# Four small reorderings in a two-layer DiT kernel: the transpose of the norm rows, one background step, the squaring of one MLP unit, and the low parts at the start of the last MLP

## The chip, the cores and the metric

The kernel runs on one core of one Trainium2 chip, in one launch. The metric is the device time of that core in microseconds; the kernel before was run three times, 1193.29, 1194.93 and 1197.53 us, median 1194.93. A compute engine executes its own instructions in order: TensorE (PE) does the matrix products and the transposes, VectorE (DVE), ScalarE (ACT) and GpSimd (POOL) the elementwise work, and SyncE (SP) issues nearly all loads. An instruction that needs another engine's result waits on a semaphore, and everything behind it on its engine waits with it.

## The reference, cut to what matters

Two transformer layers over 256 latent tokens `x` and 256 context tokens `ctx`, D = 1024. Each layer derives shifts, scales and gates from `c` (the adaLN weights `ada_w`, 25 MB a layer). Layer 0 mixes tokens with a chunked retention of 4 heads, layer 1 with neighbourhood attention of 32 heads; both are followed by a squared-relu MLP of width 4096. In layer 1 only the latents are needed.

```python
for i in range(DEPTH):
    mod = (silu_c @ ada_w[i] + ada_b[i])[:, None, :]
    mod_c = silu_cc @ ada_w[i] + ada_b[i]
    sh1, sc1, g1, sh2, sc2, g2 = jnp.split(mod, 6, axis=-1)
    h = x * (1.0 + sc1) + sh1
    hc = ctx * (1.0 + sc1c) + sh1c
    y, yc = retention_mixer(...) if i % 2 == 0 else neighbourhood_mixer(...)
    x = layer_norm(DN_ALPHA * x + g1 * y, ln_g[i, 0], ln_b[i, 0])
    h = x * (1.0 + sc2) + sh2
    x = layer_norm(DN_ALPHA * x + g2 * sq_relu_mlp(h, mlp_w1[i], mlp_w2[i]), ln_g[i, 1], ln_b[i, 1])
    # layer 0 does the same for ctx

def finish(o, g):      # the end of the retention: gates g, output weights w_o
    on = (of - mu) * lax.rsqrt(var + LN_EPS)
    return (on * jax.nn.silu(g)) @ w_o

def sq_relu_mlp(h, w1, w2):
    return jnp.square(jax.nn.relu(h @ w1)) @ w2
```

## The kernel before, in words

**Products.** Everything is fp32. A product is done as three matmuls of a reduced fp32 form: high part by high part, high by low, low by high (`mm3`). A weight unit of 512 KB is loaded by SP into one of four `raw` buffers (`fetch`), ACT casts it to `hi`, and DVE subtracts to get `lo` (`lows`; until then the cast is in the list `pending`). Only after `lo` is the raw buffer free for the next load. The adaLN chunks `rawa` take their buffers from the same four.

**Tokens.** 512 tokens stand in four tiles of 128: tiles 0 and 1 are latents, 2 and 3 context. Their transposed high and low parts are `hTh` and `hTl`.

**Order.** Each engine's calls go through `InOrder` (line 84, which is why every row of the profile says L84); where its switch is on, the engine's instructions keep the order of the program text, elsewhere a scheduler places them. PSUM has eight banks (`bank`), given out in turn: a new tile waits until the last reader of the bank's former tile is done.

**First stage.** While the first weights stream in, each of eight chunks `k` of the input is transposed, modulated and projected (`pq`, `pv`). `ln_columns` belongs to none of them: it transposes rows of norm weights and adaLN biases on PE (`pc`), copies them to `lnT` and `acol` on DVE, and stores a scaled copy through POOL. It stands in chunk 5.

**Retention heads.** For each head `h` the order on PE is q and k, v, scores, gates, states and outputs `po`, output projection `pw`. `gates((2, 3))` computes the gate inputs `pg` of the context tiles, `gate(0)` and `gate(1)` those of the latents. DVE normalizes `po` to `gs`, ACT makes silu's factor `sg` from `pg`, POOL multiplies (`gs<-sg,gs`), PE transposes the product (`pT`), ACT and DVE split it into `oh` and `ol` for `pw`. Beside it runs the background stream `bg()`: each step loads the next adaLN chunk on SP and weighs the one before with four `strips` instructions on DVE; after a group of chunks a reduction `red` and a small PE product `pada` give a group of columns. In head 0, each of the gate calls makes steps at k = 3: two until the first gate row is ready, one after.

**Layer 0's MLP.** Eight groups of hidden units (`fp`), each with two banks `p1` (a half of 128 hidden units each, latents in the left 256 columns, context in the right). The first two groups start on the latents alone, while the context tiles are still being normalized (`affine`, `mod_high`); then `evac1` squares the latents (relu on ACT, `scalar_tensor_tensor` on DVE into `r`, split into `hid` high and low), and `ctx_mm1` writes the context columns of the same banks.

**Layer 1's start of the MLP.** The last norm (`moments`, the reciprocal root on POOL, `shift_of`, `center` giving `xn`), the transposes `pt`, the affine that gives `hTh` and `hTl` (`affine_half` for tile 0, `direct` with `low1` for tile 1), and `tok_part`: the products of the first unit, tile by tile and part by part into `p00`, `p01`, `p10`, `p11` (`p1t` in the profile).

Of the kernel before, what the change touches and what calls it, by code (L numbers as in the profile page):

```python
# [19 lines left out]
KC = D // P  # L20
# [84 lines left out]
def kernel(  # L105
# [842 lines left out]
    w = ws[0]  # L948
# [8 lines left out]
    for k in range(KC):  # L957
        if k == 0:
            dt = slot(S_VL, [P, 4, 384], F32, "dt")
            sp.dma_start(out=dt[:, 0], in_=dist)  # L960
        if k == 3:
            sp.dma_start(out=cst1[:], in_=consts[:, NC0:])
            lrows = ln_rows()
        if k:
            chunk_q(k, ((0, 0),))
            part_v(k, 0, 0)
            chunk_q(k, ((1, 0), (0, 1)))
        if k < KC - 1:
            for i in range(2):
                chunk_sums(k + 1, i)  # L970
            chunk_turn(k + 1)
            ws[k + 1].high()
            chunk_row(k + 1)
            if k > 2:
                ws[k + 1].low()
        if k < 4:
            chunk_loads(k + 4)
        part_v(k, 1, 0)
        if k < KC - 1:
            chunk_columns(k + 1)  # L980
            chunk_modulate(k + 1, lambda: None if k > 2 else ws[k + 1].low())
        part_v(k, 0, 1)
        if k == 1:
            tabs = strip_tables(dt)
        if 1 < k < 6:
            make_strip(k - 2, *tabs)
        if k == 5:
            ln_columns(lrows)
        if k > 5:
            take(0, 2 * (k - 5))  # L990
# [54 lines left out]
    for h in range(RH):  # L1045
# [34 lines left out]
        def gates(ts, between=()):  # L1080

            pgs = [bank("pg") for _ in ts]
            for k in range(KC):
                wh, wl = gu[k // 2]
                for t, pg in zip(ts, pgs):
                    mm3(pg[:], hs(k, t * P, (t + 1) * P), (wh[:, k % 2, :], wl[:, k % 2, :]), k == 0, k == KC - 1)
                if h == 0 and k == 3:
                    bg(2 if G1s[0] is None else 1)
                    first_gate()
                if k in between:  # L1090
                    between[k]()
            return pgs
# [177 lines left out]
            stat(3, 1)  # L1270
            m3 = moments(3)

    def relu_sq(ps, sl, hh, hl):
        w = sl.stop - sl.start
        r = scr("r")
        act.activation(out=r[:, :w], in_=ps[:, sl], func=AF.Relu)
        dve.scalar_tensor_tensor(
            out=r[:, :w], in0=ps[:, sl], scalar=0.0, in1=r[:, :w], op0=ALU.max, op1=ALU.mult
        )
        split(r[:, :w], hh, hl)  # L1280


    HS = [S_T0, S_T1, S_SH, S_SL, S_TH, S_TL, S_GS, S_VH]
# [25 lines left out]
    for hf in range(2):  # L1309
# [9 lines left out]
        if hf == 0:  # L1319
            us = take(2, 2, 1)  # L1320
            pbs = [[bank("p1") for _ in range(2)] for _ in range(2)]
            hts = [hslot(fp) for fp in range(2)]
            mm1(us, LAT, pbs[0], range(0, 4))
            lows(1)
            shift = shift_of(*m3)
            f2 = affine(2, turn(2))
            fetch(1)
            low21 = mod_high(f2[1], 1, 2)
            white(3, shift, m3[1])
            low20 = mod_high(f2[0], 0, 2)  # L1330
            mm1(us, LAT, pbs[0], range(4, KC))
            lows(1)
            low21()
            us += take(2, 2)
            mm1(us[2:4], LAT, pbs[1], range(0, 4))
            p3 = turn(3)
            mm1(us[2:4], LAT, pbs[1], range(4, KC))
            f3 = affine(3, p3)
            low20()
            low31, low30 = (mod_high(f3[half], half, 3) for half in (1, 0))  # L1340
            low31()
            low30()
            take(0, 1)
            for fp in range(2):
                evac1(pbs[fp], LAT, hts[fp])
            for e in ORDER[1:]:
                e.on = False
            for fp in range(2):
                ctx_mm1(us[2 * fp : 2 * fp + 2], pbs[fp])
                evac1(pbs[fp], CTX, hts[fp])  # L1350
            hid += hts
            outside()
# [595 lines left out]
    settle_last(0, 1, wo_parts(0, 1))  # L1948
    mv0, r0 = moments(0)
    wo_first(1, 1, HALVES)  # L1950
    lows(1)
    fetch(1)
    shift = shift_of(mv0, r0)
    center(0, 0, mv0, r0, x0, shift)
    center(0, 1, mv0, r0, x0)
    fetch(1)
    settle_last(1, 0, wo_last(1, 0))

# [19 lines left out]
    def direct(pts, t):  # L1978
# [15 lines left out]
            part(half == 0, half, lambda k, i: hi[:, k])  # L1994

        def low(half):
            part(half == 1, half, lambda k, i: tmps[half][:, tsl(i)])
            ks = slice(4 * half, 4 * half + 4)
            dve.tensor_sub(
                out=lo[:, ks], in0=tmps[half][:].rearrange("p (k t) -> p k t", k=4), in1=hi[:, ks].bitcast(F32)  # L2000
            )
# [43 lines left out]
    HH, HL, LH = (0, 0), (0, 1), (1, 0)  # L2045
    tok_part(p00, 0, 0, *HH, LOW, start=True)
    tok_part(p00, 0, 0, *HL, LOW)
    tok_part(p00, 0, 0, *HH, HIGH)
    tok_part(p01, 0, 1, *HH, LOW, start=True)
    tok_part(p01, 0, 1, *HH, HIGH)  # L2050
    tok_part(p00, 0, 0, *LH, LOW)
    tok_part(p01, 0, 1, *LH, LOW)
# [14 lines left out]
    tok_part(p10, 1, 0, *HH, HIGH)  # L2067
    tok_part(p10, 1, 0, *HL, HIGH)
    tok_part(p01, 0, 1, *HL, LOW)
    low1(1)  # L2070
    lows(1)
    tok_part(p11, 1, 1, *HH, start=True)
    tok_part(p10, 1, 0, *LH, HIGH)
    tok_part(p01, 0, 1, *HL, HIGH, stop=True)
    low1(0)
    fetch(1)
    r00 = activate(p00)
# [166 lines left out]
```

## Time and profile before

| | |
|---|---|
| runs | 1193.29, 1194.93, 1197.53 us (median 1194.93) |
| profiled execution | 1193.21 us, its span 1191.4 us |
| granted TensorE clock | 0.998 |
| instructions | 17865 |
| bytes moved by DMA | 193.16 MB, mean 162 GB/s |

The profile shows one execution. A timeline row gives start and busy time in us, engine, line, operation, output and inputs by the program's names, and in square brackets the idle time of the engine just before it with what ended that. A row with x4 is four like instructions; its time is that of all four. The waits list gives total, times and longest. The stretches give length, then busy time and count for PE, PEld (PE's weight load), DVE, ACT and POOL, the clock, the DMA engines' share and GB/s.

### The profile page before, as it was taken

The page shows a single profiled execution, that of the slowest core. Times are in us where ns is not written, and L with a number is a line of the kernel's source. Part 1 is how long each engine was busy: PE and PEld are TensorE (multiplying, and loading weights), DVE is VectorE, ACT ScalarE, POOL GpSimd, SP SyncE. Part 2 cuts the span into 40 slices and gives each one's busy share as a digit, 9 for nine tenths or more (in the row PEclk, how much of TensorE's full clock was granted, in tenths as well). Part 3 has the DMA queues.
Part 4 walks back from the last instruction along what each step waited for, and adds up shares of the span by engine and source line. Part 5 has one row for each costly group of instructions (what it writes and reads, how often), then busy time and mean ns, then how long its engine had stood idle before and what let it go on. Part 6 is the DMA issues. An engine that isn't in the chain of part 4 may idle for free.

```text
span 1191.4 us, 17865 instructions
## 1 busy us (share of the span) xinstructions
PE 1175.3 (99%) x6884; PEld 987.6 (83%) x6884; DVE 833.5 (70%) x1308; ACT 479.4 (40%) x809; POOL 246.7 (21%) x389
## 2 busy tenths in 40 slices
PE   9999999999999999999999999999999999999997
PEld 7777888888888888888888888889778878999886
DVE  3776985777587477568867675578566688986446
ACT  3652232232223146442112333137466666666341
POOL 0103301310320141690203000123444431000001
PEclk9999999999999999999999999999999999999999
DMA  9964442444244115756566665556244334676661
GB/s 278 268 234 156 153 148 74 129 137 140 90 157 143 65 60 174 217 120 197 177 208 195 197 210 182 192 154 200 82 142 133 100 117 155 208 220 195 228 211 38
DMA packets 138041, 193.16 MB, mean 162 GB/s; under 512 B 9772, under 2 KB 81108, under 8 KB 137956
## 3 DMA queue, kind: packets, MB, share of 16 engines
q1 hardware_dynamic: 129572, 179.02, 47.3%
q0 software_dynamic: 7232, 10.44, 3.8%
q10 hardware_dynamic: 1152, 2.56, 0.7%
q8 instruction: 54, 0.88, 0.3%
q14 instruction: 31, 0.25, 0.1%
HBM read 187.15 MB, written 5.75 MB: 162 GB/s over the span
## 4 chain that ended last, share of the span: by engine, by line
PE 92%; DVE 3%; ACT 2%; issue 2%; POOL 1%; DMA 0%; DVEq 0%; POOLq 0%; ACTq 0%
PE p L84 43%; PE pq L84 8%; PE pv L84 7%; PE pw L84 7%; PE pg L84 7%; PE pn L84 5%; PE pnv L84 4%; PE po L84 2%; PE pada L84 2%; PE pS L84 1%; PE ppt L84 1%; PE pqk L84 1%; PE pav L84 1%; PE pt L84 1%; ACT s L84 1%
## 5 line engine op out<-in xcount | busy, mean ns | idle before, releaser
L84 ACT CAST hi<-raw 128x1024 fp32r<-128x1024 f32 (+2 forms) x228 | 232.6, 1033 | 323.7 <-PE p L84 117.7
L84 DVE TENSOR_TENSOR lo<-raw,hi 128x1024 fp32r<-128x1024 f32 (+2 forms) x228 | 279.8, 1238 | 94.1 <-ACT hi L84 93.3
L84 PE MATMUL p<-hi,hid 128*128 128x512 f32 (+1 forms) x832 | 241.7, 373 | 0.0
L84 PEld LDWEIGHTS p<-hi,hid 128*128 128x128 f32 x832 | 152.1, 188 | 27.6
L84 PE MATMUL p<-hTh,lo 128*128 128x256 f32 (+1 forms) x512 | 165.8, 326 | 0.0
L84 PE MATMUL p<-hTl,hi 128*128 128x256 f32 (+1 forms) x512 | 165.8, 326 | 0.0
L84 PE MATMUL p<-hTh,hi 128*128 128x256 f32 (+1 forms) x512 | 163.2, 328 | 2.5 <-DVE r L84 2.4
L84 PE MATMUL p<-lo,hid 128*128 128x512 f32 (+1 forms) x416 | 155.2, 373 | 0.0
L84 DVE SCALAR_TENSOR_TENSOR acc<-rawa,scol,acc 128x1024 f32<-128x1024 f32 x56 | 74.8, 1346 | 66.0 <-DMA rawa<-in_ada_w_dram 65.9
L84 PEld LDWEIGHTS p<-hTh,hi 128*128 128x128 f32 x512 | 94.2, 188 | 11.6 <-DVE r L84 2.9
L84 PEld LDWEIGHTS p<-hTh,lo 128*128 128x128 f32 x512 | 96.4, 188 | 8.8
L84 PEld LDWEIGHTS p<-hTl,hi 128*128 128x128 f32 x512 | 96.4, 188 | 8.7
L84 POOL TENSOR_TENSOR R<-R,acc 128x512 f32<-128x512 f32 x40 | 58.5, 1476 | 208.4 <-DVE acc L84 208.4
L84 PEld LDWEIGHTS p<-lo,hid 128*128 128x128 f32 x416 | 78.4, 188 | 13.7
L84 ACT CAST hid<-r 128x256 fp32r<-128x256 f32 (+1 forms) x64 | 31.9, 500 | 104.9 <-DVE r L84 104.9
L84 POOL TENSOR_TENSOR rstd<-rstd,misc 128x1 f32<-128x1 f32 x28 | 20.1, 718 | 213.3 <-DVE rstd L84 212.2
L84 DVE SCALAR_TENSOR_TENSOR strips<-rawa,scol,strips 128x512 f32<-128x512 f32 x84 | 61.4, 786 | 0.0
L84 ACT ACTIVATE s<-s,mn 128x512 f32<-128x512 f32 x64 | 45.5, 712 | 26.2 <-DVE mn L84 26.2
L84 PE MATMUL pg<-hi,hTh 128*128 128x512 f32 x128 | 51.4, 402 | 0.0
L84 PE MATMUL pw<-hi,oh 128*128 128x512 f32 x128 | 50.9, 398 | 0.0
L84 PE MATMUL pw<-hi,ol 128*128 128x512 f32 x128 | 50.1, 391 | 0.8 <-DVE ol L84 0.8
L84 PE MATMUL pg<-hi,hTl 128*128 128x512 f32 x128 | 50.0, 390 | 0.0
(238 smaller groups left out, 2281.1 us busy)
## 6 DMA issues: line engine op xcount, KB each, us to landing
raw<-in_mlp_w_dram SPq DMA_DIRECT2D x128, 512.0 KB, 4.4
rawa<-in_ada_w_dram SPq DMA_DIRECT2D x80, 512.0 KB, 4.2
raw<-in_ret_w_in_dram SPq DMA_DIRECT2D x42, 512.0 KB, 3.6
raw<-in_nat_w_in_dram SPq DMA_DIRECT2D x24, 512.0 KB, 4.0
rawq<-in_ada_w_dram SPq DMA_DIRECT2D x16, 512.0 KB, 6.0
raw<-in_ret_w_o_dram SPq DMA_DIRECT2D x16, 512.0 KB, 4.1
bias<-rpb_rows POOLq DMA_DIRECT2D x32, 128.0 KB, 2.9
raw<-in_nat_w_o_dram SPq DMA_DIRECT2D x8, 512.0 KB, 4.2
```

What stands on the lines that cost most here:

```text
L84: r = f(*args, **kwargs)
```

## The change

Four places.

1. `ln_columns` is called in the last chunk (k = 7) in place of chunk 5.
2. In head 0, `gates((2, 3))` makes no background step; `gate(0)` and `gate(1)` make two each as before. The number of steps in the program is the same, so the steps behind it each weigh the chunk that the step before them used to weigh.
3. `relu_sq` is cut in two: `squared` does the relu and the square, `split` follows. For the first group of layer 0's MLP, `squared` is called for both halves before `affine(3, ...)`, the split after it.
4. At layer 1's last norm, `lows(1)` moves behind the centring of tile 0; `low1` does its affine wholly on ACT; `p01`'s first part goes ahead of `p00`'s second, `p01`'s last part ahead of one of `p10`'s; and `lows(1)` goes ahead of `low1(1)`.

```diff
-        if k == 5:
+        if k == KC - 1:
             ln_columns(lrows)
...
-                if h == 0 and k == 3:
-                    bg(2 if G1s[0] is None else 1)
+                if h == 0 and k == 3 and len(ts) == 1:
+                    bg(2)
                     first_gate()
...
-    def relu_sq(ps, sl, hh, hl):
+    def squared(ps, sl):
         w = sl.stop - sl.start
         r = scr("r")
         act.activation(out=r[:, :w], in_=ps[:, sl], func=AF.Relu)
         dve.scalar_tensor_tensor(
             out=r[:, :w], in0=ps[:, sl], scalar=0.0, in1=r[:, :w], op0=ALU.max, op1=ALU.mult
         )
-        split(r[:, :w], hh, hl)
+        return r[:, :w]
+
+    def relu_sq(ps, sl, hh, hl):
+        split(squared(ps, sl), hh, hl)
...
             mm1(us[2:4], LAT, pbs[1], range(4, KC))
+            r0 = [squared(pb, LAT) for pb in pbs[0]]
             f3 = affine(3, p3)
...
-            for fp in range(2):
-                evac1(pbs[fp], LAT, hts[fp])
+            for i in range(2):
+                split(r0[i], hts[0][:, i, 0, LAT], hts[0][:, i, 1, LAT])
+            evac1(pbs[1], LAT, hts[1])
...
     wo_first(1, 1, HALVES)
-    lows(1)
     fetch(1)
     shift = shift_of(mv0, r0)
     center(0, 0, mv0, r0, x0, shift)
     center(0, 1, mv0, r0, x0)
+    lows(1)
     fetch(1)
...
         def low(half):
-            part(half == 1, half, lambda k, i: tmps[half][:, tsl(i)])
+            part(True, half, lambda k, i: tmps[half][:, tsl(i)])
...
     tok_part(p00, 0, 0, *HL, LOW)
+    tok_part(p01, 0, 1, *HH, LOW, start=True)
     tok_part(p00, 0, 0, *HH, HIGH)
-    tok_part(p01, 0, 1, *HH, LOW, start=True)
...
+    lows(1)
     low1(1)
-    lows(1)
     tok_part(p11, 1, 1, *HH, start=True)
+    tok_part(p01, 0, 1, *HL, HIGH, stop=True)
     tok_part(p10, 1, 0, *LH, HIGH)
-    tok_part(p01, 0, 1, *HL, HIGH, stop=True)
```

What stands in DVE's queue in head 0 at the gates of the context tiles, before (`strips` weigh the adaLN chunk `rawa`, `gs` is the normalized output, `lo` the low part of an output weight, `ol` the low part of the transposed product):

```order
L84 TENSOR_SCALAR gs_893<-po_1106,mv_1115,rstd_1117 128x512 [waits DVE_49,Pool_49]
L84 TENSOR_SCALAR strips_118<-rawa_1061,scol,strips_118 128x512 [waits DMAHW6_49]
L84 TENSOR_SCALAR strips_119<-rawa_1061,scol,strips_119 128x512
L84 TENSOR_SCALAR strips_118<-rawa_1061,scol,strips_118 128x512 [waits DVE_49]
L84 TENSOR_SCALAR strips_119<-rawa_1061,scol,strips_119 128x512 [waits DVE_49]
L84 TENSOR_TENSOR lo_1202<-raw_1199,hi_1201 128x1024 [waits DMAHW0_49,Activation_49]
L84 TENSOR_TENSOR lo_1208<-raw_1205,hi_1207 128x1024 [waits DMAHW1_49,Activation_49]
L84 TENSOR_TENSOR ol_1122<-pT_1161,oh_1121 128x4x128 [waits Activation_49]
```

And now:

```order
L84 TENSOR_SCALAR gs_893<-po_1106,mv_1115,rstd_1117 128x512 [waits DVE_49,Pool_49]
L84 TENSOR_TENSOR lo_1196<-raw_1193,hi_1195 128x1024 [waits DMAHW7_49,Activation_49]
L84 TENSOR_TENSOR lo_1202<-raw_1199,hi_1201 128x1024 [waits DMAHW0_49,Activation_49]
L84 TENSOR_TENSOR ol_1122<-pT_1155,oh_1121 128x4x128 [waits Activation_49]
L84 TENSOR_TENSOR lo_1208<-raw_1205,hi_1207 128x1024 [waits DMAHW1_49,Activation_49]
L84 TENSOR_TENSOR ol_1122<-pT_1168,oh_1121 128x4x128 [waits Activation_49]
L84 TENSOR_TENSOR lo_1214<-raw_1211,hi_1213 128x1024 [waits DMAHW2_49,PE_49,Activation_49]
```

The four strips of the chunk `rawa_1061` are gone from in front of the low parts; they come behind the last `ol` of this head.

DVE's queue around the affine of the fourth tile in layer 0's MLP, before (`aff` is the affine of a transposed tile, `r` the squared relu, `hid` its low part):

```order
L84 TENSOR_TENSOR hTl<-aff_3887,hTh 128x4x128 [waits Activation_49]
L84 TENSOR_SCALAR aff_3984<-pt_3950,AB_3591 128x128 [waits PE_49]
L84 TENSOR_SCALAR aff_3984<-pt_3950,AB_3591 128x128 x3
L84 TENSOR_TENSOR hTl<-aff_3882,hTh 128x4x128 [waits Activation_49]
L84 TENSOR_TENSOR hTl<-aff_3989,hTh 128x4x128 [waits Activation_49]
L84 TENSOR_TENSOR hTl<-aff_3984,hTh 128x4x128 [waits Activation_49]
L84 TENSOR_TENSOR lo_4002<-raw_3999,hi_4001 128x1024 [waits DMAHW7_49,Activation_49]
L84 TENSOR_SCALAR r_4005<-p_638_3839,r_4005 128x256 [waits Activation_49]
L84 TENSOR_TENSOR hid_3843<-r_4005,hid_3843 128x256 [waits Activation_49]
L84 TENSOR_SCALAR r_4010<-p_639_3840,r_4010 128x256 [waits Activation_49]
```

And now:

```order
L84 TENSOR_TENSOR hTl<-aff_3887,hTh 128x4x128 [waits Activation_49]
L84 TENSOR_SCALAR r_3984<-p_638_3839,r_3984 128x256 [waits Activation_49]
L84 TENSOR_SCALAR r_3987<-p_639_3840,r_3987 128x256 [waits Activation_49]
L84 TENSOR_SCALAR aff_3990<-pt_3950,AB_3591 128x128 [waits PE_49]
L84 TENSOR_SCALAR aff_3990<-pt_3950,AB_3591 128x128 x3
L84 TENSOR_TENSOR hTl<-aff_3882,hTh 128x4x128 [waits DVE_49]
L84 TENSOR_TENSOR hTl<-aff_3995,hTh 128x4x128 [waits Activation_49]
L84 TENSOR_TENSOR hTl<-aff_3990,hTh 128x4x128 [waits Activation_49]
L84 TENSOR_TENSOR lo_4008<-raw_4005,hi_4007 128x1024 [waits DMAHW7_49,Activation_49]
L84 TENSOR_TENSOR hid_3843<-r_3984,hid_3843 128x256 [waits Activation_49]
```

The two squarings `r` of the first group stand ahead of the affine of tile 3 and of a weight's low part, where they stood behind both; on ACT their relus go ahead of that engine's half of the affine likewise.

DVE's queue at the norm of tile 0 in layer 1, before (`mv` are the moments, `rstd` the argument of POOL's root, `nmr` the shift that needs the root's result):

```order
L84 TENSOR_SCALAR rstd_9042<-mv_9040 128x1 [waits DVE_49]
L84 TENSOR_TENSOR lo_9022<-raw_9019,hi_9021 128x1024 [waits DMAHW1_49,Activation_49]
L84 TENSOR_SCALAR nmr_9077<-mv_9040,rstd_9042 128x1 [waits Pool_49]
L84 TENSOR_SCALAR xn_8965<-R_104,mv_9040,rstd_9042 128x512
L84 TENSOR_TENSOR acc_9099<-pnw_9086,G_6873 128x512 [waits PE_49]
```

And now:

```order
L84 TENSOR_SCALAR rstd_9042<-mv_9040 128x1 [waits DVE_49]
L84 TENSOR_SCALAR nmr_9076<-mv_9040,rstd_9042 128x1 [waits Pool_49]
L84 TENSOR_SCALAR xn_8965<-R_104,mv_9040,rstd_9042 128x512
L84 TENSOR_TENSOR lo_9022<-raw_9019,hi_9021 128x1024 [waits DMAHW1_49,Activation_49]
L84 TENSOR_TENSOR acc_9099<-pnw_9086,G_6873 128x512 [waits PE_49]
```

The low part that stood between the root's argument and its first user now stands behind `xn`.

## The prediction, made before the changed kernel ran

> **What bounds the kernel now.** I read the page's table of busy times first: one engine is never free.
>
> ```profile
> PE 1175.3 (99%) x6884; PEld 987.6 (83%) x6884; DVE 833.5 (70%) x1308; ACT 479.4 (40%) x809; POOL 246.7 (21%) x389
> ```
>
> TensorE (PE) is busy 1175.3 of 1191.4 us, so the kernel gets faster by work taken from PE or by waits of PE that go. The change takes no matmul away; only waits are left. Next the list of what PE waited for (total, times, longest, in us):
>
> ```profile
> PE p L84 <- DVE r L84: 2.4, 1, 2.4
> PE pT L84 <- POOL gs L84: 1.5, 1, 1.5
> PE pw L84 <- DVE ol L84: 0.8, 1, 0.8
> PE pt L84 <- ACT xn L84: 0.6, 1, 0.6
> PE pc L84 <- PE pv L84: 0.5, 1, 0.5
> ```
>
> Each happens once; two waits of 0.3 and less for `p1t` follow further down. The timeline puts all seven into four stretches, so I asked for busy times by stretch (length, then busy time of PE, PEld, DVE, ACT, POOL, the clock, DMA share, GB/s):
>
> ```profile
> 49.00:76.00 27.00, 26.54 (x163) 19.92 (x161) 24.55 (x48) 18.41 (x28) 0.00 (x0) 1.00 0.77 245
> 76.00:105.00 29.00, 29.00 (x159) 21.91 (x158) 14.07 (x26) 6.94 (x10) 6.18 (x10) 1.00 0.60 203
> 105.00:121.00 16.00, 13.77 (x66) 10.75 (x65) 12.36 (x15) 5.89 (x8) 5.42 (x8) 1.00 0.39 132
> 121.00:450.00 329.00, 328.94 (x1534) 272.94 (x1533) 245.71 (x374) 97.83 (x142) 69.97 (x75) 1.00 0.37 119
> 450.00:468.00 18.00, 15.54 (x129) 15.13 (x128) 13.62 (x29) 12.40 (x25) 1.95 (x2) 1.00 0.41 140
> 468.00:990.00 522.00, 521.54 (x3079) 432.56 (x3078) 358.70 (x566) 217.57 (x408) 149.21 (x276) 1.00 0.55 168
> 990.00:1020.00 30.00, 28.83 (x207) 26.27 (x207) 26.80 (x51) 17.96 (x36) 2.42 (x2) 1.00 0.46 144
> 1020.00:1184.00 164.00, 163.92 (x1145) 152.18 (x1143) 106.55 (x142) 79.96 (x119) 3.99 (x3) 1.00 0.58 188
> ```
>
> Length less PE's busy time is PE's idle: 0.46, 2.23, 2.46 and 1.17 us in the four stretches that the change touches, 6.32 together. Between and behind them PE idles 0.00, 0.06, 0.46 and 0.08 us, so what is gained in one stretch is kept in the next as long as nobody else becomes late. A wait costs a little more than its idle time, because the overlap of successive matmuls is lost too:
>
> ```profile
> 112.11 0.39 PE L84 MATMUL pw<-hi,oh 128*128 128x512 f32 x1
> 112.33 0.39 PE L84 MATMUL pw<-lo,oh 128*128 128x512 f32 x1
> 113.48 0.50 PE L84 MATMUL pw<-hi,ol 128*128 128x512 f32 x1 [0.76 <-DVE ol L84]
> ```
>
> Starts are 0.22 apart while it runs and 1.15 at the wait: 0.93 lost where the row says 0.76, some 0.16 more. Seven waits make 1.1, so the ceiling of the whole change is about 7.4 us.
>
> **Part A, the norm rows' transpose two chunks later.** PE now waits 0.46 us for the PSUM bank of `pc`; with the 0.16 it is worth 0.62. Behind the last chunk the transpose stands between two projections and the bank has long been free. What is added: the copy to `lnT` and the two `acol` adds now stand in DVE's queue between the second and third of four low parts.
>
> ```profile
> 52.52 0.22 DVE L84 COPY lnT<-pc 128x64 f32<-128x64 f32 x1
> 52.66 0.26 DVE L84 TENSOR_SCALAR acol<-pc 128x24 f32<-128x24 f32 x2
> ```
>
> ```profile
> 77.93 1.23 DVE L84 TENSOR_TENSOR lo<-raw,hi 128x1024 fp32r<-128x1024 f32 x1 [1.81 <-ACT hi L84]
> ```
>
> The three take about 0.5 us by their starts, and DVE will wait a little for the transpose, an estimated 0.1, so everything behind them on DVE is some 0.6 later: two low parts, the rotation of q and k, and the loads that SP may issue only when DVE has freed a buffer. The cover is the 1.81 us that DVE idles before 77.93, and that PE idles 0.00 between 76 and 105 us; the last adaLN chunk's matmuls moreover stand four matmuls (0.9 us) later on PE. If that cover fails, the loss is at most the 0.6 us shift, which makes the part zero. Between 0 and 0.6 I take 0.4, nearer to the end that the 1.81 speaks for.
>
> **Part B, one background step fewer in head 0's gates of the context tiles.** The step loads an adaLN chunk on SP and weighs the previous one with four strips on DVE.
>
> ```profile
> 107.82 2.73 DVE L84 SCALAR_TENSOR_TENSOR strips<-rawa,scol,strips 128x512 f32<-128x512 f32 x4
> ```
>
> ```profile
> 114.05 1.05 ACT L84 CAST hi<-raw 128x1024 fp32r<-128x1024 f32 x1 [3.93 <-DMA raw<-in_ret_w_o_dram]
> 115.00 1.08 ACT L84 ACTIVATE sg<-pg 128x512 f32<-128x512 f32 x2
> ```
>
> ```profile
> 115.68 3.06 POOL L84 TENSOR_TENSOR gs<-sg,gs 128x512 f32<-128x512 f32 x2 [8.82 <-ACT sg L84]
> ```
>
> ```profile
> 216.83 2.55 POOL L84 TENSOR_TENSOR gs<-sg,gs 128x512 f32<-128x512 f32 x2 [7.30 <-ACT sg L84]
> ```
>
> ```profile
> 117.53 0.66 PE L84 MATMUL pT<-cst,gs 128*128 128x128 f32 x4 [1.47 <-POOL gs L84]
> ```
>
> Two chains hang on it. The strips delay the low parts and with them `ol`, for which PE waits 0.76. And they free the buffer into which SP loads the last output weight: ACT stands 3.93 us before its cast, both gate activations `sg` are queued behind that cast, POOL's product waits 8.82, and PE waits 1.47 for its transposes. Without the step that load takes the buffer of the chunk weighed one step before, and no longer waits for these strips; the gates run as soon as PE has finished them, which is before the 112.11 of the first `pw`. So `sg` starts near 111.6, over 3 us earlier, and the first product, half of the pair's 2.55 to 3.06, is done between 113.5 and 114. PE asks for it today at 117.53 less 1.47, and without the `ol` wait 0.93 earlier: 115.1. The dropped step falls to a later head, and every later step of the stream slides by one. Heads 1 to 3 already had the one-step order in these gates and show no wait there. Both waits with their restarts are 2.55; I take 2.4 and as the low end 0.9, only the `ol` wait.
>
> The product's two rows say what could hold it: the pair took 3.06 us in head 0, beside a low part on DVE, and 2.55 in head 1. The Trainium skill, "SBUF — State Buffer", section "Who interferes with whom", says that a DVE instruction with two SBUF inputs and a GpSimd one that reads SBUF exclude each other, the later one blocking fully; the trace agrees with a delay of that kind. By that rule the low parts that move next to the product could hold the first product for one whole low part, 1.2 us (the row at 77.93), to 115.2 at worst: level with PE's asking, and the sum would lose 0.1.
>
> **Part C, the first unit's latents squared ahead of tile 3's affine.** The largest single wait. PE wants to write the context columns of a bank of which DVE has still to read the latent columns.
>
> ```profile
> 460.67 2.44 PE L84 MATMUL p<-hTh,hi 128*128 128x256 f32 x16 [2.45 <-DVE r L84]
> ```
>
> ```profile
> 455.40 1.51 ACT L84 ACTIVATE aff<-pt,AB 128x128 f32<-128x128 f32 x4 [1.33 <-PE pt L84]
> 456.94 1.14 ACT L84 CAST hTh<-aff 128x512 fp32r<-128x512 f32 x2
> ```
>
> ```profile
> 455.07 1.36 DVE L84 TENSOR_SCALAR aff<-pt,AB 128x128 f32<-128x128 f32 x4
> ```
>
> ```profile
> 459.06 1.23 DVE L84 TENSOR_TENSOR lo<-raw,hi 128x1024 fp32r<-128x1024 f32 x1 [0.17 <-ACT hi L84]
> 460.20 0.42 DVE L84 SCALAR_TENSOR_TENSOR r<-p,r 128x256 f32<-128x256 f32 x1
> ```
>
> Reading DVE backwards: `r` at 460.20 stands behind a low part, which stands behind a cast, which stands behind the fourth tile's casts, none of which it needs. Now two relus (estimated as long as the squarings, 0.42 each) run on ACT in the 1.33 that it idles, and two squarings on DVE just ahead of its affine, which ends some 0.7 later, near 457.1; the second of the two casts starts only near 457.5 as it is. So the casts still end at 458.08; PE is ready at 460.67 less 2.45 and the restart, 458.06. What is left of the wait is nil to 0.1. The second unit's bank is asked for 48 matmuls later, some 7 us at the row's 0.15 each, and freed earlier than now. 2.45 plus 0.16, less 0.1: I take 2.45. The low end, if the squarings push the affine past the cast, is 1.75.
>
> **Part D, the start of the last MLP.** A single low part moves off POOL's reciprocal root, one affine goes from DVE to ACT, and PE takes parts whose operands are ready first.
>
> ```profile
> 997.89 1.50 POOL L84 TENSOR_TENSOR rstd<-rstd,misc 128x1 f32<-128x1 f32 x1 [11.88 <-DVE rstd L84]
> ```
>
> ```profile
> 403.80 0.57 POOL L84 TENSOR_TENSOR rstd<-rstd,misc 128x1 f32<-128x1 f32 x1
> ```
>
> ```profile
> 1000.54 1.09 PE L84 MATMUL pt<-cst,xn 128*128 128x128 f32 x8 [0.55 <-ACT xn L84]
> ```
>
> The same root takes 0.57 where DVE runs nothing beside it, so xn comes 0.9 earlier, more than the 0.55 that PE waits. The other waits in the stretch's 1.17, for `hTh` and `hTl` of `p1t`, are met by the order of the parts and by ACT's affine. With three restarts the 1.17 is about 1.7; I leave 0.1 for a rest at the last half: 1.6, low end 0.7 (the first wait alone).
>
> **Sum.** 0.4 + 2.4 + 2.45 + 1.6 = 6.85 us. The profiled execution took 1193.21, so the changed kernel's would take 1186.4. The median of the three runs is 1194.93, 1.72 above that; the predicted median is 1188.1.
>
> **Rivals.** (1) One of the two large waits stays or only moves. For C: the relus and squarings wait for matmuls of the second unit, and nothing is freed early; then 2.45 less, 1190.5. For B: ACT's casts still stand ahead of the gates; then 1.5 less, 1189.6. For it speaks that queues are in order and a single late item blocks all; against it that both chains have a margin of about 1 us. Chance 0.15. (2) The weights bind: the last MLP reads 188 GB/s, and the low part moved in D comes behind `xn`, an estimated 1.3 us later, and frees its buffer so much later. If the stream set the pace from there, D's 1.6 would become a loss of 1.3: 1191.0. Against it: the DMA engines' share there is 0.58, where the stretch from 49 to 76 moved 245 GB/s, and PE idles 0.08 in 164 us. Chance 0.05. (3) Slower: since the stream of steps slides by one, the adaLN columns of heads 1 and 2 stand directly ahead of PE's `po`, and DVE's queue behind them.
>
> ```profile
> 196.76 8.16 PE po L84 x36
> ```
>
> ```profile
> 191.16 0.17 DVE L84 TENSOR_TENSOR mod<-pada,acol 128x16 f32<-128x16 f32 x1 [3.47 <-PE pada L84]
> 191.25 0.87 DVE L84 TENSOR_SCALAR strips<-rawa,scol 128x512 f32<-128x512 f32 x2
> 192.04 4.06 DVE L84 SCALAR_TENSOR_TENSOR strips<-rawa,scol,strips 128x512 f32<-128x512 f32 x6
> 199.52 0.70 DVE L84 BATCH_NORM_STATS2 bs<-po 128x6 f32<-128x512 f32 x1 [3.42 <-PE po L84]
> ```
>
> Today `mod` runs at 191, eight strips follow, and DVE idles 3.42 before the first `bs`. Changed, the columns are turned where `po` starts, `mod` comes near 197.1, and one step's four strips follow, 0.8 us and a third of 4.06: 199.3, just in time for 199.52. If the chunk that they weigh lands late, `bs`, the products and PE follow one for one, twice. To eat 6.85 it must cost 3.4 in each head, that is land after some 201; to be slower by over 0.3% it must cost 5.2. Against it: the strips at 192.04 show no wait for their chunk today. Chance 0.05, time about 1199.
>
> **How the numbers follow.** The forecast has 0.75; 0.15, 0.05 and 0.05 go to the rivals. The range begins at the ceiling of 7.4 taken from a run 2 us under the median, 1185.0, and reaches over rivals (1) and (2) and the terms' low ends (0 + 0.9 + 1.75 + 0.7 = 3.35, which is 1191.6) to 1192.5. A measurement of this kernel can tell about 0.3%, 3.6 us, from no change, so faster means below 1191.3. The forecast, nearly all of it, and rival (1) fall there: 0.84. Rival (2) and several low ends at once are the same: 0.11. The rest is slower: 0.05.
>
> **What would show it.** Right: PE's waits for `r`, `gs`, `ol`, `xn` and `pc` gone from the list; idle in the four stretches under 1 us together; `sg` near 111; `r` for the first unit near 455.5 (less what was gained before); the root at 998 near 0.57. Wrong: a wait of PE for `pada` or `red` ahead of `po`; waits on loads in the last MLP; a PE wait for the hTh cast near 456 of more than 0.3; a new wait for adaLN chunks near 78.

## The result, and the profile after

The changed kernel takes 1186.26 us (median of 6 runs, 1185.87 to 1188.63), the kernel before, run beside it, 1194.24 (6 runs, 1193.29 to 1197.53): ratio 0.9935, 95% interval 0.9920 to 0.9951, 7.98 us less. The profiled execution is 1188.31 us, its span 1186.5; before it was 1193.21. So the medians fell by 8.0 and the profiled executions by only 4.9, and the reading has to explain both.

TensorE's list of waits is the first view again. These three rows are the whole list now; none is left of the seven that the change aimed at, and the three waits stood there before (the second with 0.4).

```profile
PE pq L84 <- DVE still L84: 1.2, 1, 1.2
PE pq L84 <- ACT hTh L84: 0.3, 1, 0.3
PE pqk L84 <- ACT pt L84: 0.3, 1, 0.3
```

The stretches agree (length, then busy time of PE, PEld, DVE, ACT, POOL, the clock, DMA share, GB/s). PE idles 0.00, 0.00, 0.00 and 0.14 us in the four places, where it idled 0.46, 2.23, 2.46 and 1.17.

```profile
49.00:76.00 27.00, 27.00 (x167) 20.10 (x170) 24.21 (x47) 18.60 (x28) 0.00 (x0) 1.00 0.78 245
104.50:118.00 13.50, 13.50 (x70) 11.18 (x68) 9.52 (x11) 5.90 (x8) 5.79 (x8) 1.00 0.45 146
440.00:468.00 28.00, 28.00 (x224) 27.41 (x223) 24.12 (x47) 20.91 (x39) 4.16 (x4) 1.00 0.51 151
980.00:1013.00 33.00, 32.86 (x258) 30.20 (x256) 29.75 (x57) 22.53 (x46) 1.50 (x2) 1.00 0.50 157
```

Where the time went is read best from the chain that ended last, by pieces that both kernels have (start, length, engine, output). They stand behind part A (head 0), behind B (heads 1 and 3), behind C (layer 0's MLP), ahead of D, and behind D (the last MLP). Before:

```profile
80.57 4.18 PE pS L84 x24
181.28 4.18 PE pS L84 x24
384.67 4.18 PE pS L84 x24
587.17 49.19 PE p L84 x216
813.84 14.54 PE pn L84 x120
1024.59 159.35 PE p L84 x1104
```

After:

```profile
80.16 4.18 PE pS L84 x24
178.06 4.18 PE pS L84 x24
381.45 4.18 PE pS L84 x24
580.98 49.19 PE p L84 x216
807.65 14.54 PE pn L84 x120
1016.92 162.12 PE p L84 x1104
```

The starts differ by 0.41, 3.22, 3.22, 6.19, 6.19 and 7.67 us. So A brought 0.41 in this execution, B 2.81, C 2.97 and D, by these pieces, 1.48; between the places less than 0.1 was gained or lost. Compared matmul by matmul, D brought 1.73 by 1017 us of before, just ahead of the last MLP's first product; the matmuls there are 7.85 earlier, and a slower pace takes 0.2 of that back by the last start. Then the last piece, the same 1104 matmuls, took 2.77 us longer. That alone makes 7.67 into 4.9; the experiments below show that it isn't the change's doing.

The moved instructions on the timeline (start, busy time, engine, operation, output and inputs, and in brackets the idle time before it). In head 0's gates of the context tiles the first gate activation, at 115.00 before, and POOL's product, at 115.68 before:

```profile
111.21 1.34 ACT L84 ACTIVATE sg<-pg 128x512 f32<-128x512 f32 x2 [0.99 <-PE pg L84]
111.89 2.55 POOL L84 TENSOR_TENSOR gs<-sg,gs 128x512 f32<-128x512 f32 x2 [5.44 <-ACT sg L84]
```

At the first unit of layer 0's MLP, relus and squarings in the gaps, and the cast that used to stand in front of them:

```profile
450.74 0.65 ACT L84 ACTIVATE r<-p 128x256 f32<-128x256 f32 x2
...
453.71 1.14 ACT L84 CAST hTh<-aff 128x512 fp32r<-128x512 f32 x2
```

```profile
451.83 0.75 DVE L84 SCALAR_TENSOR_TENSOR r<-p,r 128x256 f32<-128x256 f32 x2
452.50 1.36 DVE L84 TENSOR_SCALAR aff<-pt,AB 128x128 f32<-128x128 f32 x4
```

That cast was at 456.94: 3.23 earlier, all of what A and B had gained by then, so the squarings delay nothing. And the root of the last norm:

```profile
991.79 0.57 POOL L84 TENSOR_TENSOR rstd<-rstd,misc 128x1 f32<-128x1 f32 x1 [11.90 <-DVE rstd L84]
```

### The profile page after: what moved, and what is told of

It reads as the page before. It is cut to its first block, busy times and chain, and to the rows that moved or that the text cites. A ratio compares the mean times of both kernels' runs of the same rounds, so it can differ in the third digit from the quotient of the medians.

```text
span 1186.5 us, 17867 instructions
## 1 busy us (share of the span) xinstructions
PE 1176.7 (99%) x6884; PEld 990.9 (84%) x6884; DVE 832.8 (70%) x1304; ACT 480.9 (41%) x813; POOL 248.9 (21%) x389
## 4 chain that ended last, share of the span: by engine, by line
PE 96%; ACT 1%; DVE 1%; issue 1%; DMA 0%; POOL 0%; DVEq 0%; ACTq 0%
PE p L84 44%; PE pq L84 8%; PE pg L84 7%; PE pv L84 7%; PE pw L84 7%; PE pn L84 5%; PE pnv L84 4%; PE po L84 3%; PE pada L84 2%; PE pnw L84 1%; PE pS L84 1%; PE ppt L84 1%; PE pqk L84 1%; PE pt L84 1%; PE pav L84 1%; PE p1t L84 1%
## 5 line engine op out<-in xcount | busy, mean ns | idle before, releaser
L84 POOL TENSOR_TENSOR R<-R,acc 128x512 f32<-128x512 f32 x40 | 62.2, 1565 | 212.3 <-DVE acc L84 212.2
L84 DVE SCALAR_TENSOR_TENSOR strips<-rawa,scol,strips 128x512 f32<-128x512 f32 x84 | 66.4, 847 | 0.0
L84 PE MATMUL pg<-lo,hTh 128*128 128x512 f32 x128 | 50.0, 391 | 0.0
```

What stands on the lines that cost most here:

```text
L84: r = f(*args, **kwargs)
```

## The experiments

Of the single parts and of the whole I look at two things: the ratio of times, and the shift of PE's matmuls against the kernel before, matmul by matmul, just ahead of and just behind the place. Only the second tells parts of 0.4 to 3 us apart, because executions start up to 4.3 us apart. Most of that lies ahead of 20 us and goes with the granted clock, the share of full speed that TensorE's clock is allowed: its record has 1.00 from 5.4 us on in the profile of before, from 10.8 in that of C alone and from 17.6 in that of D alone, and at 20 us the latter two are 1.75 and 4.32 late.

### Each part alone

**A alone.**

```diff
-        if k == 5:
+        if k == KC - 1:
             ln_columns(lrows)
```

> Only the norm rows' transpose moved to the last chunk. Theory (the terms of the four parts add up, each by the PE wait it removes): PE's wait for pc (0.46 us, 0.62 with the restart) is gone, and PE reaches the second gate of head 0 about 0.4 us earlier than before; all other waits stay as before, the time falls by 0.4 us, too little to be told by time alone. Rival (the 0.6 us that DVE loses at 60 us comes back as a PE wait for the adaLN chunks near 76 to 79): gain 0 by 105 us.

1197.28 us against 1195.37, ratio 1.0009 (0.9998 to 1.0020): no gain. The wait for `pc` is gone and PE is 0.45 us earlier behind the moved transpose, at 62 us, but the list of waits has a row that wasn't there before:

```profile
PE pada L84 <- DMA rawa<-in_ada_w_dram: 0.2, 1, 0.2
```

By 105 us 0.24 is left of the 0.45.

**B alone.**

```diff
-                if h == 0 and k == 3:
-                    bg(2 if G1s[0] is None else 1)
+                if h == 0 and k == 3 and len(ts) == 1:
+                    bg(2)
```

> Only the background step in head 0's context gates dropped. Theory: PE's waits for ol (0.8) and gs (1.5) are both gone, PE is 2.4 to 2.8 us earlier at 130 us and keeps it to 450 us; the time falls by about 2.6 us. Rival 1 (POOL's product held by DVE's low parts): the gs wait shrinks but 0.5 us or more of it stays, gain under 2. Rival 2 (the slid background stream makes heads 1 and 2 late at po): a PE wait for red or po inputs near 196 and 298, gain at 450 us smaller than at 130 us.

1192.61 us, ratio 0.9980 (0.9967 to 0.9994). The waits for `ol` and `gs` are gone, and PE's shift goes from +1.54 at 101 us to -1.26 at 130: 2.80. It stays -1.26 up to 450 us, through `po` of heads 1 and 2, so the slid steps cost those heads nothing.

**C alone.** (`squared` for both halves ahead of `affine(3, p3)`, as in the change's diff.)

```diff
+            r0 = [squared(pb, LAT) for pb in pbs[0]]
             f3 = affine(3, p3)
```

> Only the first unit's latents squared ahead of tile 3's affine. Theory: PE's wait for r (2.4 us) is gone and none takes its place; PE is 2.5 to 3.0 us earlier at 480 us; the time falls by 2.5 to 3.0 us. Rival (the wait moves to the fourth tile's hTh cast or to the second unit's bank): a wait of 0.4 to 0.8 us stays near 458 or 464, gain under 2.2.

1191.74 us, ratio 0.9974 (0.9963 to 0.9985). The wait for `r` is gone, none takes its place, and the shift goes from +1.63 to -1.33: 2.96.

**D alone.** (All its edits at layer 1's last norm, as in the change's diff.)

```diff
-    lows(1)
     fetch(1)
...
     center(0, 1, mv0, r0, x0)
+    lows(1)
```

> Only the start of the last MLP reordered. Theory: the waits for xn, hTh and hTl are gone, POOL's root near 998 takes 0.55 to 0.6 us in place of 1.50, PE is 1.5 us earlier at 1022 us. In the stretch 1024 to 1094 us of 256-column matmuls the pitch of one matmul was 113.3 ns in the kernel before and 117.8 ns in the changed one. Theory 1 (the pitch is a state that varies from run to run, whatever the kernel): these four kernels show both values without relation to the edit. Theory 2 (the reordered start sets it): 117.8 here, 113.3 in the three kernels with the old start; then this kernel's time is 1.5 less 2.9, that is about 1.4 us slower than before.

1195.74 us, ratio 0.9991 (0.9978 to 1.0003): too small to be told by the time. In the trace the waits for `xn`, `hTl` and `hTh` are gone, and the shift goes from +5.40 to +3.67: 1.73.

### What makes each wait

**The dropped step behind the gates instead of nowhere.** The step is kept in head 0, but made after both products of the gates.

```diff
-                if h == 0 and k == 3:
-                    bg(2 if G1s[0] is None else 1)
+                if h == 0 and k == 3 and len(ts) == 1:
+                    bg(2)
...
+        if h == 0:
+            bg(1)
```

> Kernel before, but head 0's step of the context gates is made behind the gates and their products in the program, not left out: DVE's strips stand behind both ol, SP's order of loads stays. It separates the two chains of part B. Theory (the strips hold ol; the buffer that they free holds the third output weight, its cast, sg and POOL's product): the ol wait (0.8) goes, the gs wait stays, 1.0 to 1.8 us, since the third load now waits for the first low part's buffer, near 109, and PE asks for gs 0.9 earlier; PE is 0.9 to 1.4 us earlier at 130 us, about half of the 2.8 of the step dropped. Rival (DVE's queue is all there is to it, the load doesn't matter): both waits go, 2.8 us at 130 us.

1195.62 us in one execution; PE ends 0.42 us behind at 130, where 0.9 to 1.4 ahead was expected: a miss, but one that shows how the queue works. The first `ol` is early as foreseen, and PE is 0.92 ahead at 113. The load of the last output weight now waits for the buffer of the first low part and goes out at 109.57 instead of 110.58; ACT's cast still stands 4.28 us for it, with the gates behind it, so the wait for `gs` stays. And the four strips now stand in front of the third `ol`. DVE's rows, and PE's:

```profile
115.96 4.19 DVE L84 SCALAR_TENSOR_TENSOR strips<-rawa,scol,strips 128x512 f32<-128x512 f32 x4
121.81 0.68 DVE L84 TENSOR_TENSOR ol<-pT,oh 128x512 fp32r<-128x512 f32 x1
```

```profile
116.63 0.66 PE L84 MATMUL pT<-cst,gs 128*128 128x128 f32 x4 [1.13 <-POOL gs L84]
122.54 0.50 PE L84 MATMUL pw<-hi,ol 128*128 128x512 f32 x1 [1.60 <-DVE ol L84]
```

So the strips in DVE's queue and the load in ACT's are two separate chains, as part B had them, and moving the step just behind the gates isn't enough.

**The context columns in banks of their own.** Nothing is squared earlier; the matmuls that waited write elsewhere.

```diff
-                ctx_mm1(us[2 * fp : 2 * fp + 2], pbs[fp])
-                evac1(pbs[fp], CTX, hts[fp])
+                pbc = [bank("p1") for _ in range(2)]
+                ctx_mm1(us[2 * fp : 2 * fp + 2], pbc)
+                evac1(pbc, CTX, hts[fp])
```

> Kernel before, nothing moved, but the context columns of the first two groups of layer 0's MLP go to PSUM banks of their own. Theory (PE waits at 458 us for the readers of the bank, not for data): the wait for r is gone or under 0.2 us, PE is 2.6 to 4.1 us earlier at 470 us, as with the squaring moved. Rival (PE waits for the high parts of the fourth tile or for DVE as such): a wait of 1 us or more stays at 458 us.

1196.59 us in one execution, whose start was 4.2 late. The wait for `r` is gone with `r` as late as ever, and the shift goes from +6.27 to +3.31: 2.96, the same as for C alone. (Of the +6.27, 2.04 were lost at head 0's wait for `gs`, which lasted 1.98 in this execution; the edit doesn't touch that place.) The wait was for the bank, not for data.

**Half of D: only `lows(1)` behind the centring of tile 0.**

```diff
-    lows(1)
     fetch(1)
     shift = shift_of(mv0, r0)
     center(0, 0, mv0, r0, x0, shift)
     center(0, 1, mv0, r0, x0)
+    lows(1)
```

> Only one of the edits at the last norm: the single low part moved from beside POOL's reciprocal root to behind the centring. Theory (a low part on DVE holds the root): the root near 998 takes 0.55 to 0.60 us in place of 1.50, the wait for xn (0.5 to 0.6) is gone, the two waits for p1t stay, PE is 0.7 to 0.8 us earlier at 1002 us and no more at 1018. Rival (the root's length has another cause): it stays near 1.5, and PE gains nothing.

**The other half: all of D but that line** (`low1`'s affine on ACT and the order of the parts).

```diff
-            part(half == 1, half, lambda k, i: tmps[half][:, tsl(i)])
+            part(True, half, lambda k, i: tmps[half][:, tsl(i)])
...
```

> The edits at the last norm without the moved low part: ACT's affine, the order of the products' parts, and the last low part ahead of low1. Theory (each removes its own wait): the root near 998 takes about 1.5 us again and PE waits 0.5 to 0.6 for xn; the waits for hTh (0.2) and hTl (0.3) are gone, PE is 0.7 to 1.0 us earlier at 1022 us than at 1000 us, compared with the kernel before; with d_root's 0.76 this makes the 1.6 to 1.7 of all edits together. Rival (the parts need each other: without the earlier root the later waits come back): under 0.4 us.

One execution each, 1196.89 and 1194.01 us. POOL's root, in the first and in the second:

```profile
999.36 0.57 POOL L84 TENSOR_TENSOR rstd<-rstd,misc 128x1 f32<-128x1 f32 x1 [11.89 <-DVE rstd L84]
```

```profile
999.48 1.50 POOL L84 TENSOR_TENSOR rstd<-rstd,misc 128x1 f32<-128x1 f32 x1 [11.90 <-DVE rstd L84]
```

With the low part gone from beside it the root takes 0.57 and PE's wait for `xn` goes: PE gains 0.76 by 1002 us. Without that edit the root and that wait stay and the waits for `hTl` and `hTh` go. Read at 1017 us, ahead of the last MLP's first product, the halves bring 0.74 and 0.97; the two make 1.71, D alone made 1.73.

### The whole, with and without part A

**The changed kernel again**, for a comparison on one chip with the next kernels.

> The changed kernel once more, for its time beside the kernel before in many runs, and for a second profile. Theory (the four waits are gone for good, with them the fall of the granted clock at 460 us; what is left between runs is the start and the pitch of 113.3 or 117.8 ns in the last MLP): 7.5 to 9 us less than before by the medians, a ratio of 0.9925 to 0.994, no PE wait over 0.4 us behind the first 15 us, no clock under 1.00 near 455 us. If the pitch is 113.3 this time, PE ends some 7.7 us earlier than in the profile of before, less what the start differs. Rival (the changed start of the last MLP brings the pitch of 117.8 with it): 117.8 again, though the edit alone had 113.3.

1187.17 us (1186.99 to 1190.90, 5 runs), ratio 0.9940 (0.9928 to 0.9953), as expected. Two expectations failed: PE waits 1.0 us for an adaLN chunk near 79 us, and in the profile its last product starts 6.0 us earlier than before, not 7.7. The pace of the last MLP is the fast one this time.

**The change without A.**

```diff
-        if k == KC - 1:
+        if k == 5:
             ln_columns(lrows)
```

> The changed kernel with the norm rows' transpose left in chunk 5. Theory (part A is worth its wait, 0.4 to 0.5 us, and nothing else): PE's wait for pc is there again (0.4 to 0.5), PE is 0.2 to 0.5 us later at 130 us than in the changed kernel for the same start, and the time is 0.2 to 0.5 us above it, within the noise. Rival (DVE's lost 0.6 us at 60 us costs PE an adaLN wait in many runs, as in the one profile of the edit alone): the time is the same or lower than the changed kernel's, by up to 0.5 us.

1186.04 us (1185.79 to 1186.37), ratio 0.9926 (0.9912 to 0.9939). The ratios' intervals overlap, but each of its five runs is below each of the five with A: the version with A takes 1.1 us longer here. That is the rival's direction, and more than the 0.5 that it allowed. Between the two profiles lie 1.3 us. By the shifts 0.15 of it was there at 49 us, 0.6 comes at part A's place, and 0.55 at 776 us, where only the profile with A has a wait of PE for a low part; whether that one has to do with A is open. In the profile with A, PE's matmuls of the fourth chunk of adaLN's weights:

```profile
79.96 0.64 PE L84 MATMUL pada<-rawa,cT 128*32 128x256 f32 x8 [1.04 <-DMA rawa<-in_ada_w_dram]
```

and before, without a wait:

```profile
78.33 0.64 PE L84 MATMUL pada<-rawa,cT 128*32 128x256 f32 x8
```

The cause is seen on SP's queue (start and time, the loads with like ones put together). With A, and then before:

```profile
72.50 0.38 SPq L84 DMA_DIRECT2D raw<-in_ret_w_o_dram  x1
72.97 8.88 SPq L84 DMA_DIRECT2D rawa<-in_ada_w_dram  x5
```

```profile
71.69 0.38 SPq L84 DMA_DIRECT2D raw<-in_ret_w_o_dram  x1
72.88 7.36 SPq L84 DMA_DIRECT2D rawa<-in_ada_w_dram  x5
```

The output weight's load goes out 0.81 later, right in front of the chunk's load, because the two have changed the buffers that they wait for. Before, the first was released by a low part on DVE at 71.68 and the second by PE's adaLN matmuls at 72.87. With A the first waits for PE's adaLN matmuls, until 72.49; the low part on DVE was done at 72.16, so the second follows at once. (Why the buffers change places is open.) The chunk is issued 0.09 later but lands, by the trace, at 79.92 in place of 78.07: 6.95 us under way instead of 5.2. The same is seen in all three profiles with the transpose in the last chunk: the two loads go out 0.47 apart and the chunk takes 5.82, 6.09 and 6.95 us, where in the other eleven they go out 1.2 apart and it takes 4.64 to 5.56. Before, PE asked for it 0.26 us after its landing; there was no more margin than that. In the first profile of the changed kernel the chunk landed at 78.80 and PE asked at 78.86: just in time, hence the 0.41 there.

**The rows turned after head 0's second gate** (a third place for A's step, far from the loads).

```diff
-        if k == 5:
-            ln_columns(lrows)
...
+            ln_columns(lrows)   # behind gate(1) of head 0
```

> The changed kernel with part A's call put elsewhere: the norm rows are transposed behind head 0's second gate, at about 92 us, where DVE is about half idle, and neither in chunk 5 nor in chunk 7. Theory (part A removes PE's wait for pc but pays by DVE's 0.5 to 0.6 us at 60 us, which bunches the loads so that the adaLN chunk that PE asks for at 78 lands late): no wait for pc, no wait for rawa at 78 us beyond 0.1, PE 0.4 to 0.6 us earlier at 105 us than in the kernel before for the same start; about 0.4 us below the kernel without part A, a ratio of 0.992 to 0.9925. Rival (the wait of 1.0 us for rawa came by chance and can come in any kernel): a wait for rawa of 0.2 to 1.0 us near 78 us here as well.

1186.12 us (1185.66 to 1188.73, 6 runs), ratio 0.9926 (0.9911 to 0.9942). Neither the wait for `pc` at 50 us nor the one for the chunk is there, the two loads go out 1.20 apart again, and PE gains 0.46 by 105 us. The time doesn't show it: the same as without A within the scatter, where 0.4 less was expected. By their ratios these two versions are the best that ran, though the intervals overlap with the changed kernel's.

### The clock behind the wait

**Twenty idle matmuls in the wait for `r`**: the wait stays, but PE is not idle in it. The matmuls write a bank that nobody reads.

```diff
+            fill = bank("fill")
+            for _ in range(20):
+                pe.matmul(fill[:, LAT], lhsT=us[0][0][:, 0, tsl(0)], rhs=hTh[:, 0, LAT], start=True, stop=True)
```

> Kernel before with 20 idle matmuls (256 columns, result unused) put where PE waits 2.45 us for r at 458 us; the wait's reason is untouched. In the kernel before and three others with this wait the granted clock fell after it: 0.5 in the records, a pitch of 213 to 222 ns for 2 to 14 matmuls in place of 120; in the two kernels without the wait it did not. Theory (PE's idleness lowers the clock): no matmul slower than 125 ns after the filled stretch, PE 0.3 to 1.4 us earlier at 470 us than in the kernels with the wait, although it still starts the context columns no earlier than 460.7 less shifts. Rival (the slow matmuls come from DVE and ACT reading banks at that time): the pitch near 213 stays.

1195.25 us against 1197.42, ratio 0.9991 (0.9972 to 1.0011): not told apart by the time. The traces say why it was tried. With part A alone, where the wait is as before, the two microseconds behind it have a granted clock of 0.50 (the third figure from the end):

```profile
461.00:463.00 2.00, 2.00 (x11) 2.00 (x11) 1.52 (x4) 0.94 (x3) 0.28 (x1) 0.50 0.78 216
```

and with the idle matmuls

```profile
461.00:463.00 2.00, 1.99 (x15) 1.78 (x16) 1.26 (x4) 1.21 (x4) 0.01 (x1) 1.00 0.61 182
```

Six of the seven profiles with the wait show the clock fall to 0.50 behind it: 11 to 14 matmuls start every 0.21 us instead of 0.12, and PE loses 1.0 to 1.4 us. The profile of before is the seventh, without a fall; the expectation above wrongly counts it among the others. None of the seven profiles in which PE has no idle there shows it, the one with the idle matmuls included.

Why one profile escapes can be read off the traces. Each fall in the middle of a kernel lasts 3.41 us in the clock's record, and from the first record at 1.00 to a fall it is a whole number of times 3.413 us (453.97, or 133 times, with A alone). So the clock is set for one window of 3.41 us after another, and the windows' edges lie elsewhere in each execution. Cut at these edges, the stretches around the wait with A alone, around the same wait before, and around head 0's wait for `gs` with D alone (the figure behind the length is PE's busy time):

```profile
456.83:460.24 3.41, 1.31 (x11) 1.10 (x10) 2.67 (x5) 2.37 (x4) 0.00 (x0) 1.00 0.20 68
460.24:463.65 3.41, 3.07 (x14) 3.07 (x15) 2.00 (x6) 2.01 (x6) 0.52 (x1) 0.50 0.54 154
```

```profile
455.98:459.39 3.41, 2.24 (x19) 2.04 (x17) 2.68 (x6) 3.29 (x7) 0.00 (x0) 1.00 0.43 141
459.39:462.81 3.42, 2.12 (x15) 1.92 (x16) 2.48 (x6) 1.38 (x4) 0.00 (x1) 1.00 0.35 108
```

```profile
119.97:123.38 3.41, 1.87 (x11) 1.34 (x10) 2.22 (x2) 2.07 (x3) 3.06 (x2) 1.00 0.77 251
123.38:126.80 3.42, 3.42 (x19) 2.84 (x18) 3.05 (x5) 0.59 (x1) 1.98 (x2) 1.00 0.52 175
```

With A alone most of the wait falls into one window, PE is busy for 1.31 us of it, and the next window is at 0.50. Before, counted from its record at 5.42 us, an edge at 459.39 cuts the wait in two, and neither half is enough. In all fourteen profiles, between 16 and 1170 us, seven windows have PE busy for 1.50 us or less, and each is followed by one at 0.50; no other is, and the least busy of the others has 1.87. One of the seven is head 0's wait for `gs` in the run with other banks, 1.98 us long.

### The longer last piece

No kernel was made for this; all fourteen profiles answer. In the last MLP's first product, 256-column matmuls one after another, the stretch from 1030 to 1080 us of before, of after, and of the changed kernel run again:

```profile
1030.00:1080.00 50.00, 50.00 (x444) 50.00 (x443) 41.50 (x62) 32.27 (x58) 0.00 (x0) 1.00 0.67 211
```

```profile
1030.00:1080.00 50.00, 50.00 (x426) 50.00 (x426) 38.20 (x57) 30.32 (x53) 0.00 (x0) 1.00 0.60 190
```

```profile
1030.00:1080.00 50.00, 50.00 (x444) 50.00 (x443) 38.99 (x59) 30.90 (x57) 0.00 (x0) 1.00 0.64 201
```

PE is busy throughout at a granted clock of 1.00, yet sets off 444 matmuls or 426: one every 113 or 118 ns. Ten profiles have the first pace, four the second (after, B alone, C alone, and D's half with the root), and the same changed kernel has both. All fourteen begin this product at 118 ns; the ten change over between 1018 and 1026 us. So it goes by the execution, and the 2.77 us are no part of the change. What sets the pace is open.

## Why the prediction was right

**The total** of 1188.1 against 1186.26 was right in its mechanism for parts B, C and D, which make nearly all of it, and missed 1.84 by sizes that partly cancel. The terms against the earlier starts of PE's work (before less after):

| part | predicted | profile of the whole | alone |
|---|---|---|---|
| A | 0.4 | 0.41 | 0.24 |
| B | 2.4 | 2.81 | 2.80 |
| C | 2.45 | 2.97 | 2.96 |
| D (at 1017 us) | 1.6 | 1.73 | 1.73 |
| sum | 6.85 | 7.92 | 7.73 |

**Part A: the step that failed.** The prediction named the place ("a new wait for adaLN chunks near 78") and a delay on DVE, but bounded a failed cover by "at most the 0.6 us shift". DVE's rows after show a wait of 0.63 for the transpose where 0.1 was estimated; with the three instructions DVE loses 1.04 us, of which 0.54 had been gained ahead of it:

```profile
60.18 0.22 DVE L84 COPY lnT<-pc 128x64 f32<-128x64 f32 x1 [0.63 <-PE pc L84]
60.32 0.26 DVE L84 TENSOR_SCALAR acol<-pc 128x24 f32<-128x24 f32 x2
```

The loss was not bounded by the shift: two loads changed the buffers that they wait for, went out bunched and took longer on their way, up to 6.95 us in place of 5.2, so that PE waited up to 1.04. The 1.81 us that DVE idled ahead of a low part was cover for DVE's work and said nothing of the loads. Between the two whole kernels the version with A is 1.1 us slower, of which the profiles put 0.6 at this place; in the first profile of the changed kernel A gained 0.41, and alone its ratio is 1.0009 with no change inside the interval. So A brings nothing that the time shows, and 0.4 was luck where it came.

**Part B was right, and undersized.** `sg` came at 111.21 (predicted 111.6), the first of the pair's products was done before PE asked, and both waits went. The prediction counted 0.16 for each restart. The traced starts of before give more: behind `ol` 0.93 and then a first matmul of 0.33 where 0.23 is usual; behind `gs` 1.86 where 0.23 is usual, 1.63, and again 0.08 in the next. That is 2.74 of the 2.81. POOL's pair took 2.55: that a low part of DVE would block it, as the Trainium skill's rule on shared ports ("SBUF — State Buffer", "Who interferes with whom") made possible, did not come about here. It was the other way round: DVE's low part at 113.53, behind the start of POOL's second product, took 2.00 where others take 1.22, and nobody waited for it. The root was held as the rule has it, 1.50 against 0.57.

**Part C was right, and undersized by 0.5.** PE could have gone on at 458.06 and did at 460.67, 2.61 lost. Then 16 matmuls of the first bank and its neighbour took from 460.67 to 462.95, 2.28 in place of 16 x 0.12: another 0.36. By their single starts 0.10 of it is the slow first matmul, 0.17 a second, shorter wait at the second half's bank (461.61 to 461.90), which the list of waits doesn't show, and 0.11 the slow first matmul behind that. 2.61 and 0.36 are the 2.97. The squarings cost the affine nothing.

**Part D was right**: root 0.57, waits gone, 1.73 for 1.6.

**The way from profile to median failed**, and hid it. The prediction carried the 1.72 us between the profile of before and its median over to the changed kernel. But the profile of before is the one execution with the wait in which the clock did not fall behind it, so a loss of 1.0 to 1.4 that the other six profiles have was not in its rows; and the profile after fell on the slow pace of the last MLP. Profiled, the gain is 4.9, by medians 8.0. The version without A is the plainer sum: B, C and D alone are worth 7.5, its median fell by 8.8, and the 1.3 between them has the size of one fall of the clock. The traces show the fall and which windows bring it; that it makes the rest of the medians is likely but not shown, as the idle matmuls' interval of times holds both no effect and 0.28%.

**The range.** Its lower end was added up wrongly: 1194.93 less 2 less 7.4 is 1185.5, not 1185.0. The measured time lies above both.

**The rivals.** That a large wait stays or moves: it did not, and the step made behind the gates shows what it would have been like. That the stream of weights binds in the last MLP: no wait for a load stands in the list. That heads 1 and 2 become late at `po`: B alone kept its -1.26 through both.

## What to carry to other kernels

A wait listed at 2.4 us was worth 3.0: add the restart, read off by the starts of the matmuls on both sides, look behind the wait for a second one on the next bank, and look at the granted clock behind it, which made such a wait 1.0 to 1.4 us dearer in six profiles of seven. When a step moves in an engine's queue, see which buffer each load behind it waits for, before and after, and compare each load's landing with the time at which it is asked for; a margin of 0.26 us is none. And a single profile is one draw: pieces that both kernels have in the chain show which differences are the change's and which are the execution's.

## What the runs showed of the chip that was not expected

- The granted clock was set by windows of 3.41 us whose edges differ between executions: PE busy for 1.50 us or less of a window was followed by 0.50 in the next, 1.87 or more was not. The Trainium skill ("TensorE: Matmul & The Clock Gate", Part 1, "What's actually happening") has a window of about 3.4 us that runs freely and an idle window that halves the clock. Length and free running agree with it; that a window with 1.50 us of work in it counts as idle does not follow from its words.
- The same 256-column matmuls, with the same weight loads and the clock at 1.00, run at 113 or at 118 ns each for 70 us, by the execution; it is worth 2.8 us.
- DVE's three-operand strips took 4.19 us for four beside POOL's product (the step behind the gates), where the four took 2.73 before.
